# The beginning and the latent stage of a two-layer hybrid backbone: modulation weights in tiles that are written later, products in column groups, tokens first, projections reordered

## The chip, the cores and the metric

The kernel runs on one core of a Trainium2 chip. The metric is the device time of one execution in microseconds (us). A core has TensorE (matmuls, PE in the profile; its weight loads are PEld), VectorE (DVE), ScalarE (ACT), GpSimd (POOL) and SyncE (SP), each with its own queue of instructions that runs in order, and 16 DMA engines that move data between DRAM and the on-chip memory. Transfers are issued from the queues of SP, ACT and POOL.

## The reference

The reference is a backbone of two layers over 1024 latent tokens and 256 context tokens of width 1024. Each layer computes six modulation vectors from a conditioning vector (a product with `ada_w`), normalises and modulates the tokens, and mixes them. Layer 0 mixes by latent attention and a gated linear attention side by side, layer 1 by a gated delta rule; a squared-ReLU MLP follows in each. What the change touches is the head of layer 0:

```
ml = jnp.split(jax.nn.silu(c) @ ada_w[layer] + ada_b[layer], N_MOD, axis=-1)     # and mc from c_ctx
a_lat = modulate(rms_norm(h_lat, norm1_w[layer]), ml[0], ml[1])                  # h * (1 + scale) + shift
y = a_lat @ w_in                                                                 # split into cq, ckv, kpe, gq, ...
q = rms_norm(cq, q_norm) @ w_uq
kv = rms_norm(ckv, kv_norm) @ w_ukv                                              # k_nope and v of each head
```

The context tokens go the same way with `mc`. Rotary positions are applied to `kpe` and to a part of `q`, and eight heads attend over all 1280 tokens.

## The kernel before

Activations lie transposed: 128 features on the partitions, tokens along the free dimension, in eight feature tiles `xs` and in three token blocks of 512, 512 and 256 (`BLOCKS`). Every projection is done in three matmuls, because each operand is split in a high part (a cast to fp32r) and a low part (the rest): `mm3`, lines 181 to 183. `split` (lines 167 and 170) makes the parts: the cast on ACT, the subtraction on VectorE or POOL as its caller says. `load_w` (line 174) loads a weight tile `wst` on SP's queue and splits it into `whi` and `wlo`.

A scheduler sets the order on each engine from the order in which the code is written and from when it expects operands to be ready, so instructions that are written later can stand earlier. A tile that is given new contents waits for the last reader of the old ones. Generators put in `lanes` are advanced by `pump` while projections are written, so that their work lies beside these.

**The beginning** (lines 565 to 595). `ada_first(m, half, ...)`, lines 140 to 156, makes half of one modulation vector; in this text it is one unit. It loads eight weight tiles of 128x512 (256 KB) into a pool `adaw` of six buffers (line 146), multiplies each with the two conditioning columns `sc` into a PSUM tile `py` of 2 rows (line 147), copies `py` to `evt` (line 149), turns it over with four matmuls into `adat` (line 152), and adds the bias into `mod` (line 154). Vector 1 is the scale and gives `A` (line 161), vector 0 the shift. Written order: scale unit of the first half, `x` of block 0, shift unit of the first half, statistics of `x` (`sq`, line 238, summed on VectorE and POOL, line 243; `st`, line 252; root, lines 205 to 215), spread over the partitions as `rb` (line 261), and the weights of the first projections 0 and 1. Then come two halves of the eight feature tiles: normed and modulated into `a0h` and `a0l` (lines 281 to 288), multiplied for projections 0 and 1 of block 0. Before the second half stand the other two units and the loads of `x` for blocks 1 and 2. Projection 3 of block 0 is done by itself afterwards, beside the norm of block 1; then follow blocks 1 and 2 for all three.

**The latent stage** (lines 687 to 765). The projections 5 to 9 leave `cq` (three tiles) and `ckv` (two) in a long-lived pool with `small_t`. The stage loads the value weights in two tiles, splits all of `ckv` and then all of `cq` (line 716), applies the rotation to the shared key part (`kp`, `k2`, lines 722 to 730), then computes the values `pv` of ten token tiles (lines 737 to 739), copies each on ACT to `vo` (line 741) and stores it (line 742). Then the rotary parts of the queries are projected in two groups (`S` with `cqh`, `cql`; lines 181 to 183 again), rotated (lines 753 to 757), split into `peh` and `pel` (lines 758, 759) and stored by POOL (lines 761, 762). `gs` (line 487) is the tail of the linear attention, which still runs beside it. The attention's tiles get constant rows 96 from ACT (lines 779 to 782) and constant columns from VectorE (line 783). Its head projects keys and queries of a pair (`ckh`, `cqh`), finds the maxima by products `M` (line 857) and reductions `mx` (line 858), and then starts the scores.

## Time and profile before

| | |
|---|---|
| median of 3 runs | 3441.19 us (3430.4 to 3442.38) |
| time of the profiled execution | 3433.3 us |
| its span | 3431.6 us |
| mean granted TensorE clock | 0.971 |
| busy: PE, DVE, ACT, POOL | 95%, 62%, 34%, 30% |
| moved by DMA | 287.87 MB |

A row of the timeline has the start from the beginning of the span, the length of one instruction or of a merged group (xN), the engine, the line, the operation with output and inputs, and in brackets how long the engine had been idle and what ended that. A row of the waits has who waited for whom, the us in total, how often, and the longest. A row of the stretches has the busy time and count of PE, PEld, DVE, ACT and POOL, the granted clock, the share of the DMA engines and GB/s. The end of a matmul is modelled, and an f32 matmul is recorded as two; so the distance from one start to the next says more than its length.

### The profile page before, as it was taken

What the parts mean: (1) busy time and instruction counts of PE and PEld (TensorE: products, weight loads), DVE (VectorE), ACT (ScalarE), POOL (GpSimd) and SP (SyncE); (2) the same over time, 40 slices, a digit from 0 to 9 for tenths busy, and PEclk for the clock granted to TensorE, in tenths of its full rate; (3) what the DMA queues carried; (4) which work ended last, traced back from release to release, by engine and by line L of the source; (5) the groups of instructions that cost most, each with busy time, mean ns of one, the idle gap of its engine ahead of it and who ended that gap; (6) DMA issues with size and microseconds to landing.
All of it is one profiled execution on the core that took longest, in us unless ns stands there. A gap on an engine that the chain in (4) does not pass through costs nothing.

```text
span 3431.6 us, 48429 instructions
## 1 busy us (share of the span) xinstructions
PE 3261.4 (95%) x18676; PEld 2708.2 (79%) x18676; DVE 2114.5 (62%) x3888; ACT 1173.9 (34%) x2158; POOL 1045.7 (30%) x790
## 2 busy tenths in 40 slices
PE   8988889999899999999999998999999999999998
PEld 4876767777787888888888786777987788888887
DVE  4757536666467777777545779783765444444445
ACT  3234245666332111111211454552664311111112
POOL 2312136666221111111111343443117422212222
PEclk9998989999999999999999999999999999999999
DMA  5633133111523222222111244346454211111111
GB/s 198 199 100 90 59 111 81 30 37 39 178 69 94 82 77 82 77 79 82 50 37 37 74 105 102 84 121 154 106 108 148 68 49 49 44 50 49 44 49 62
DMA packets 284967, 287.87 MB, mean 84 GB/s; under 512 B 156424, under 2 KB 222032, under 8 KB 284736
## 3 DMA queue, kind: packets, MB, share of 16 engines
q1 hardware_dynamic: 272928, 263.53, 26.6%
q0 software_dynamic: 5760, 10.75, 1.3%
q10 hardware_dynamic: 6048, 10.49, 1.0%
q8 instruction: 147, 2.41, 0.3%
q14 instruction: 84, 0.69, 0.1%
HBM read 231.34 MB, written 53.36 MB: 83 GB/s over the span
## 4 chain that ended last, share of the span: by engine, by line
PE 58%; DVE 8%; issue 2%; ACT 2%; POOL 1%; DMA 1%; SPq 1%; DVEq 0%; ACTq 0%; POOLq 0%
PE ps L181 17%; PE ps L183 17%; PE ps L182 17%; DVE X L1399 1%; DVE tm L1397 1%; PE pa L1646 1%; PE pa L1618 1%; DVE acc L126 1%; PE pa L1629 1%; PE pb L1627 1%; PE pb L1667 1%; DVE y L1175 1%; DMA adaw<-in_adaw_dram 1%; PE adat L133 1%; PE st L252 0%
## 5 line engine op out<-in xcount | busy, mean ns | idle before, releaser
L170 POOL TENSOR_TENSOR wlo<-wst,whi 128x1024 fp32r<-128x1024 f32 (+1 forms) x192 | 453.2, 2368 | 1609.7 <-ACT whi L167 1549.3
L167 ACT CAST whi<-wst 128x1024 fp32r<-128x1024 f32 (+2 forms) x213 | 212.6, 1012 | 824.1 <-PE ps L182 766.4
L181 PE MATMUL ps<-th,whi 128*128 128x512 f32 (+1 forms) x1304 | 480.2, 368 | 5.0 <-DVE h L1070 3.4
L183 PE MATMUL ps<-th,wlo 128*128 128x512 f32 (+1 forms) x1304 | 476.9, 366 | 2.4 <-POOL wlo L170 2.4
L182 PE MATMUL ps<-tl,whi 128*128 128x512 f32 (+1 forms) x1304 | 477.9, 366 | 0.0
L1033 DVE TENSOR_TENSOR rl<-rl 128x512 f32<-128x512 f32 (+1 forms) x160 | 209.9, 1312 | 328.4 <-ACT rl L1032 328.0
L181 PE MATMUL ps<-mxh,whi 128*128 128x512 f32 (+1 forms) x1008 | 355.0, 353 | 0.0
L182 PE MATMUL ps<-mxl,whi 128*128 128x512 f32 (+1 forms) x1008 | 350.4, 348 | 0.9 <-POOL mxl L170 0.9
L183 PE MATMUL ps<-mxh,wlo 128*128 128x512 f32 (+1 forms) x1008 | 349.8, 347 | 0.0
L126 DVE SCALAR_TENSOR_TENSOR acc<-adaw,sc,acc 128x256 f32<-128x256 f32 (+1 forms) x476 | 277.1, 624 | 46.0 <-DMA adaw<-in_adaw_dram 46.0
L1070 DVE SCALAR_TENSOR_TENSOR h<-ps,mod,h 128x512 f32<-128x512 f32 (+1 forms) x384 | 243.2, 656 | 86.5 <-PE ps L183 85.1
L181 PEld LDWEIGHTS ps<-th,whi 128*128 128x128 f32 x1304 | 247.0, 189 | 49.0 <-DVE h L1070 5.3
L183 PEld LDWEIGHTS ps<-th,wlo 128*128 128x128 f32 x1304 | 246.7, 189 | 43.5 <-POOL wlo L170 3.2
L182 PEld LDWEIGHTS ps<-tl,whi 128*128 128x128 f32 x1304 | 247.2, 190 | 38.5
L1070 DVE SCALAR_TENSOR_TENSOR g<-ps,mod,g 128x512 f32<-128x512 f32 (+1 forms) x264 | 188.5, 731 | 106.3 <-PE ps L183 106.1
L182 PEld LDWEIGHTS ps<-mxl,whi 128*128 128x128 f32 x1008 | 193.3, 192 | 26.3 <-issue 1.4
L181 PEld LDWEIGHTS ps<-mxh,whi 128*128 128x128 f32 x1008 | 193.1, 192 | 26.1 <-issue 1.2
L183 PEld LDWEIGHTS ps<-mxh,wlo 128*128 128x128 f32 x1008 | 193.0, 192 | 23.4
L932 POOL TENSOR_TENSOR pl<-P,ph 128x512 fp32r<-128x512 f32 x144 | 179.3, 1252 | 90.1 <-DVE ph L931 58.1
L183 PE MATMUL ps<-m1h,wlo 128*128 128x512 f32 x512 | 203.9, 398 | 0.0
L181 PE MATMUL ps<-m1h,whi 128*128 128x512 f32 x512 | 203.8, 398 | 0.0
L182 PE MATMUL ps<-m1l,whi 128*128 128x512 f32 x512 | 203.7, 398 | 0.0
(376 smaller groups left out, 6747.0 us busy)
## 6 DMA issues: line engine op xcount, KB each, us to landing
wst<-in_w_dram SPq DMA_DIRECT2D x128, 512.0 KB, 3.6
adaw<-in_adaw_dram SPq DMA_DIRECT2D x224, 128.0 KB, 2.1
adaw<-in_adaw_dram SPq DMA_DIRECT2D x80, 256.0 KB, 5.3
wst<-in_owT_dram SPq DMA_DIRECT2D x25, 512.0 KB, 3.4
wst<-in_ewo_dram SPq DMA_DIRECT2D x16, 512.0 KB, 4.0
wY<-d_YA SPq DMA_DIRECT2D x64, 128.0 KB, 3.0
wst<-in_owo_dram SPq DMA_DIRECT2D x16, 512.0 KB, 3.5
wst<-in_ewT_dram SPq DMA_DIRECT2D x14, 512.0 KB, 7.3
```

The source lines that it names most:

```text
L126: V.scalar_tensor_tensor(out=acc[c], in0=w, scalar=sc[:, k, c:c + 1], in1=acc[c], op0=ALU.mult, op1=ALU.add)
L133: PE.matmul(pt[:, j, c:c + 1], acc[c][:, j * 128:(j + 1) * 128], ones, start=True, stop=True)
L167: S.copy(out=hi, in_=src)
L170: lo_eng.tensor_tensor(out=lo, in0=src, in1=hi.bitcast(F32), op=ALU.subtract)
L181: PE.matmul(ps, hi_w, hi_x, start=first, stop=False)
L182: PE.matmul(ps, hi_w, lo_x, start=False, stop=False)
L183: PE.matmul(ps, lo_w, hi_x, start=False, stop=last)
L932: (V if j % 4 == 3 else G).tensor_tensor(out=pl[:, :n], in0=P_[:, :n], in1=ph[:, :n].bitcast(F32), op=ALU.subtract)
L1033: V.tensor_tensor(out=r[:, :n], in0=r[:, :n], in1=r[:, :n], op=ALU.mult)
L1070: V.scalar_tensor_tensor(out=h[m][:, c0:c0 + n], in0=ps[:, :n], scalar=mod[l][:, 40 + m, c:c + 1], in1=h[m][:, c0:c0 + n], op0=ALU.mult, o ...
L1175: V.scalar_tensor_tensor(out=y[:, o0:o1], in0=src, scalar=cw[:, m, j:j + 1], in1=y[:, o0:o1], op0=ALU.mult, op1=ALU.add)
L1397: V.tensor_tensor(out=t3, in0=X[:, k + 1:, k:k + 1].to_broadcast([128, n, k]), in1=X[:, k:k + 1, :k].to_broadcast([128, n, k]), op=ALU.mult)
```

## The change

**Units.** `ada_load` (new) issues a unit's loads, into tiles of the long-lived pool that get their own contents only later: the first eight slots lie in `cq` and `ckv`, the other eight in `ckv`, `small_t` and, in two pieces of 256 columns each, in the columns of `xs` for block 2. The pool `adaw` goes. `ada_first` multiplies with `scz`, which is `sc` padded with zeros to 32 columns, and puts the eight products in turn into four groups of 32 rows of `py`, each at its own column group of the array (`tile_position`); the copy takes 128 rows, and a selector `sel` with two columns adds the groups up while it turns them over.

**Order of the beginning.** `x` of block 0 is loaded first, then the scale unit, the two weights, the shift unit and the third weight, which now has its pool early. The loads of the second half's units and of `x` for block 1 are written ahead of the first half. Projection 3 is done in the halves too, after 0 and 1. The statistics of block 1 come after the projections 0 and 1 of the second half, and its norm is run through before block 1.

TensorE at the start of the program, before: `py` are a unit's products, `adat` turns it over, `st` are the statistics of block 0, `rb` its spread root, `ps` the first projection.

```order
L147 MATMUL py<-adaw,sc 2x512 x8
L152 MATMUL adat<-ident,evt 128x2 x4
L147 MATMUL py<-adaw,sc 2x512 x8
L152 MATMUL adat<-ident,evt 128x2 x4
L252 MATMUL st<-ones,sq 128x1 x8
L147 MATMUL py<-adaw,sc 2x512
L261 MATMUL rb<-ident,rs_y 128x128 x4
L147 MATMUL py<-adaw,sc 2x512 x2
L181 MATMUL ps<-a0h_0_129,whi 128x512 x2
```

The same place after it:

```order
L158 MATMUL py<-cq_115,scz 32x512 x2
L158 MATMUL py<-cq_116,scz 32x512 x2
L158 MATMUL py<-cq_117,scz 32x512 x2
L158 MATMUL py<-ckv_118,scz 32x512 x2
L164 MATMUL adat<-sel,evt 128x2 x4
L264 MATMUL st<-ones,sq 128x1 x8
L273 MATMUL rb<-ident,rs_y 128x128 x4
L158 MATMUL py<-ckv_119,scz 32x512 x2
```

The statistics and the spread moved ahead of the second unit.

TensorE around the spread of block 1, before (`a0h_2` to `a0h_4` are feature tiles of block 0, here in projection 3):

```order
L183 MATMUL ps<-a0h_2_131,wlo 128x512
L261 MATMUL rb<-ident,rs_y 128x128 x4
L181 MATMUL ps<-a0h_3_132,whi 128x512
L182 MATMUL ps<-a0l_3_140,whi 128x512
L183 MATMUL ps<-a0h_3_132,wlo 128x512
L181 MATMUL ps<-a0h_4_133,whi 128x512
```

And after (`a0h_6` and `a0h_7` are the last feature tiles of block 0, `a0h_0_145` the first of block 1):

```order
L194 MATMUL ps<-a0l_6_143,whi 128x512
L195 MATMUL ps<-a0h_6_135,wlo 128x512
L193 MATMUL ps<-a0h_7_136,whi 128x512
L194 MATMUL ps<-a0l_7_144,whi 128x512
L195 MATMUL ps<-a0h_7_136,wlo 128x512
L273 MATMUL rb<-ident,rs_y 128x128 x4
L193 MATMUL ps<-a0h_0_145,whi 128x512 x2
```

Fifteen products of block 0 stood between the spread and block 1; now none does.

**Latent stage.** The weight pool `wa` has three buffers and is made ahead of the split tiles. The value weights are loaded without being split at once: first block 0 of `ckv` is split, then the weights, one on VectorE and one on POOL, then the rest of `ckv`, all low parts on VectorE. The splits of `cq` are written one by one between the value products. Every other copy `vo` is on VectorE. The constant rows of `Kh` and `Ql` are copied by POOL, those of `Kl` stay on ACT.

VectorE at the start of the latent stage, before (`kp`, `k` are the rotation, `ckl` and `cql` low parts, `gs` the tail of the linear attention):

```order
L722 TENSOR_TENSOR kp<-small_t,cosT 32x512
L487 SCALAR_TENSOR_TENSOR gs<-pt,gon,gs 128x512
L170 TENSOR_TENSOR ckl_3729<-ckv_118,ckh_3724 128x512
L723 TENSOR_TENSOR k_3790<-small_t,sinT 32x512
L170 TENSOR_TENSOR ckl_3729<-ckv_118,ckh_3724 128x512
L170 TENSOR_TENSOR ckl_3729<-ckv_118,ckh_3724 128x256
```

After (`wlo` is the low part of the first value weights, `vo` the copy of the first value tile):

```order
L754 TENSOR_TENSOR kp<-small_t,cosT 32x512
L182 TENSOR_TENSOR ckl_3715<-ckv_118,ckh_3713 128x512
L499 SCALAR_TENSOR_TENSOR gs<-pt,gon,gs 128x512
L182 TENSOR_TENSOR wlo<-wst,whi 128x512
L755 TENSOR_TENSOR k_3761<-small_t,sinT 32x512
L182 TENSOR_TENSOR ckl_3715<-ckv_118,ckh_3713 128x512
L182 TENSOR_TENSOR ckl_3716<-ckv_119,ckh_3714 128x512
L182 TENSOR_TENSOR ckl_3715<-ckv_118,ckh_3713 128x256
L182 TENSOR_TENSOR ckl_3716<-ckv_119,ckh_3714 128x256
L755 TENSOR_TENSOR k_3772<-small_t,sinT 32x512
L754 TENSOR_TENSOR kp<-small_t,cosT 32x512
L776 COPY vo<-pv 128x512
```

The weights' low part came to VectorE, behind `gs`; the low parts of the second `ckv` tile came from POOL in the later blocks.

Within the attention a few rows change places; after it the order of instructions is the same in both kernels on every engine.

```diff
--- before.py
+++ after.py
@@ -137,19 +137,31 @@
                 if m == src:
                     ada_scales(l, which)
 
-    def ada_first(m, half, wpool, ypool, ppool):
+    def ada_load(m, half, ws):
+
+        u = 2 * m + half
+        for k in range(KD):
+            c = u * 512
+            for w in ws[k]:
+                nc.sync.dma_start(out=w, in_=a["adaw"][0, k * 128:(k + 1) * 128, c:c + w.shape[1]])
+                c += w.shape[1]
+
+    def ada_first(m, half, ws, sel, ypool, ppool):
+
 
         u = 2 * m + half
         py = ppool.tile([128, 512], F32, name="py", tag="q")
         for k in range(KD):
-            w = wpool.tile([128, 512], F32, name="adaw", tag="adaw")
-            nc.sync.dma_start(out=w, in_=a["adaw"][0, k * 128:(k + 1) * 128, u * 512:(u + 1) * 512])
-            PE.matmul(py[:2], sc[:, k, :], w, start=(k == 0), stop=(k == KD - 1))
+            z = 32 * (k % 4)
+            c = 0
+            for w in ws[k]:
+                PE.matmul(py[z:z + 32, c:c + w.shape[1]], sel[1][:, k, :], w, start=(k < 4), stop=(k >= 4 and w is ws[k][-1]), tile_position=(0, z))
+                c += w.shape[1]
         y = ypool.tile([128, 512], F32, name="evt", tag="evt")
-        V.tensor_copy(out=y[:2], in_=py[:2])
+        V.tensor_copy(out=y, in_=py)
         pt = ppool.tile([128, 4, 2], F32, name="adat", tag="q")
         for j in range(4):
-            PE.matmul(pt[:, j, :], y[:2, j * 128:(j + 1) * 128], ident[:2, :2], start=True, stop=True)
+            PE.matmul(pt[:, j, :], y[:, j * 128:(j + 1) * 128], sel[0], start=True, stop=True)
         us = slice(u * 4, u * 4 + 4)
         V.tensor_tensor(out=mod[0][:, us, :], in0=pt, in1=adab[:, 0, us].unsqueeze(2).to_broadcast([128, 4, 2]), op=ALU.add)
         if m == 1:
@@ -563,33 +575,46 @@
             first = [(0, to_sb(small_t)), (1, to_dram(d_gq[0])), (3, to_dram(d_gk[0]))]
             pq = pool(e2, "ppq", 3, space=PSUM)
             e3 = ExitStack()
-            aw = pool(e3, "aw0", 6)
-            ada_first(1, 0, aw, evp, pq)
+            wx = pool(e2, "wx", 1)
+            sx = pool(e3, "sx")
+            sel = (sx.tile([128, 2], F32, name="sel"), sx.tile([128, KD, 32], F32, name="scz"))
+            V.tensor_reduce(out=sel[0], in_=ident.rearrange("p (g c) -> p c g", c=32)[:, 0:2, :], axis=AX.X, op=ALU.add)
+            V.memset(sel[1], 0.0)
+            V.tensor_copy(out=sel[1][:, :, 0:2], in_=sc)
+
+            late = [[x[:, j * 512:(j + 1) * 512]] for x in cq + ckv + [small_t] for j in range(2)]
+            late += [[xs[k][:, 1024:], xs[k + 1][:, 1024:]] for k in range(0, KD, 2)]
+            late = [late[:8], late[8:]]
             load_x(0)
-            ada_first(0, 0, aw, evp, pq)
+            ada_load(1, 0, late[0])
+            ada_first(1, 0, late[0], sel, evp, pq)
+            ws0 = [load_w(a["ewT"][m], wp) for m in (0, 1)]
+            ada_load(0, 0, late[1])
+            ws0.append(load_w(a["ewT"][3], wx))
             r0 = run(stat_lane(xs, c0, n, tmp, small, pq, "q", D))
             rb = spread(r0, n // 128, pp, "p")
-            ws0 = [load_w(a["ewT"][m], p) for m, p in ((0, wp), (1, wp))]
-            pss = [pp.tile([128, 512], F32, name="ps", tag="p") for _ in range(2)]
+            ada_first(0, 0, late[1], sel, evp, pq)
+            ada_load(1, 1, late[0])
+            ada_load(0, 1, late[1])
+            load_x(1)
+            pss = [pp.tile([128, 512], F32, name="ps", tag="p") for _ in range(3)]
             for half in range(2):
+                ks = range(4 * half, 4 * half + 4)
                 if half:
-                    ada_first(1, 1, aw, evp, pq)
-                    load_x(1)
-                    ada_first(0, 1, aw, evp, pq)
+                    ada_first(1, 1, late[0], sel, evp, pq)
+                    ada_first(0, 1, late[1], sel, evp, pq)
                     load_x(2)
-                    r1 = run(stat_lane(xs, 512, 512, tmp, small, pq, "q", D))
-                run(norm0(0, rb=rb, ks=range(4 * half, 4 * half + 4)))
-                for k in range(4 * half, 4 * half + 4):
-                    for w, ps in zip(ws0, pss):
-                        mm3(ps[:, :n], *colk(w, k), *a0.at(k, c0, n), k == 0, k == KD - 1)
+                run(norm0(0, rb=rb, ks=ks))
+                for ms in ((0, 1), (2,)):
+                    for k in ks:
+                        for m in ms:
+                            mm3(pss[m][:, :n], *colk(ws0[m], k), *a0.at(k, c0, n), k == 0, k == KD - 1)
+                    if half and 0 in ms:
+                        r1 = run(stat_lane(xs, 512, 512, tmp, small, pq, "q", D))
             e3.close()
-            wx = pool(e2, "wx", 1)
-            ws0.append(load_w(a["ewT"][3], wx))
             for (_, dst), ps in zip(first, pss):
                 dst(c0, n, ps)
-            nl = lane(norm0(1, r=r1))
-            dense0(first[2:], BLOCKS[:1], 0.8, 1.6, None, ws0[2:])
-            complete(nl)
+            complete(lane(norm0(1, r=r1)))
             lane(norm0(2))
             dense0(first, BLOCKS[1:2], 0.8, 1.6, None, ws0)
             drain()
@@ -685,12 +710,12 @@
 
 
     el = ExitStack()
+    wp = pool(el, "wa", 3)
     hip = pool(el, "hip")
+    ckh = [hip.tile([128, T], F32R, name=f"ckh{i}") for i in range(2)]
+    ckl = [hip.tile([128, T], F32R, name=f"ckl{i}") for i in range(2)]
     cqh = [hip.tile([128, T], F32R, name=f"cqh{i}") for i in range(3)]
-    ckh = [hip.tile([128, T], F32R, name=f"ckh{i}") for i in range(2)]
     cql = [hip.tile([128, T], F32R, name=f"cql{i}") for i in range(3)]
-    ckl = [hip.tile([128, T], F32R, name=f"ckl{i}") for i in range(2)]
-    wp = pool(el, "wa", 2)
     def proj(m, nm, kt, xh, xl, w, pp, tag):
 
         hi, lo = w
@@ -709,12 +734,19 @@
         nc.scalar.dma_start(out=sinT, in_=a["sinT"])
         tmp = pool(e2, "tmpq", 2)
         pp = pool(e2, "ppq", 4, space=PSUM)
-        wv = [load_w(a["ukvv"][:, k * 512:(k + 1) * 512], wp, 512) for k in range(2)]
-
-        for hs, hh, hl in ((ckv, ckh, ckl), (cq, cqh, cql)):
-            for (c0, n) in BLOCKS:
-                for i, x in enumerate(hs):
-                    split(x[:, c0:c0 + n], hh[i][:, c0:c0 + n], hl[i][:, c0:c0 + n], (V, G)[i % 2])
+        sts = []
+        for k in range(2):
+            sts.append(wp.tile([128, 512], F32, name="wst", tag="wst"))
+            nc.sync.dma_start(out=sts[k], in_=a["ukvv"][:, k * 512:(k + 1) * 512])
+        wv = []
+        for (c0, n) in BLOCKS:
+            for i, x in enumerate(ckv):
+                split(x[:, c0:c0 + n], ckh[i][:, c0:c0 + n], ckl[i][:, c0:c0 + n], V if c0 else (V, G)[i % 2])
+            if not c0:
+                for k in range(2):
+                    wv.append(tuple(wp.tile([128, 512], F32R, name=x, tag=x) for x in ("whi", "wlo")))
+                    split(sts[k], *wv[k], (V, G)[k])
+        later = [(cq[i][:, c0:c0 + n], cqh[i][:, c0:c0 + n], cql[i][:, c0:c0 + n], (V, G)[i % 2]) for c0, n in BLOCKS for i in range(3)]
         for (c0, n) in BLOCKS:
             cs = slice(c0, c0 + n)
             kp, k2 = (tmp.tile([32, 512], F32, name=x, bufs=1)[:, :n] for x in ("kp", "k2"))
@@ -738,7 +770,12 @@
                 PE.matmul(ps, ckh[k][:, x0], wvl, start=False, stop=False)
                 PE.matmul(ps, ckl[k][:, x0], wvh, start=False, stop=(k == 1))
             vo = tmp.tile([128, 512], F32, name="vo")
-            S.copy(out=vo, in_=ps)
+            if t % 2:
+                S.copy(out=vo, in_=ps)
+            else:
+                V.tensor_copy(out=vo, in_=ps)
+            if later:
+                split(*later.pop(0))
             nc.sync.dma_start(out=d_v[t * 128:(t + 1) * 128, :], in_=vo)
             pump(1.3)
 
@@ -776,10 +813,10 @@
     identr = at.tile([128, 128], F32R, name="identr")
     S.copy(out=identr, in_=ident)
     for i in range(3):
-        S.copy(out=Kh[i][96:97, :], in_=ident[96:97, 96:97].to_broadcast([1, T]))
+        G.tensor_copy(out=Kh[i][96:97, :], in_=ident[96:97, 96:97].to_broadcast([1, T]))
         S.activation(out=Kl[i][96:97, :], in_=ident[96:97, 96:97].to_broadcast([1, T]), func=AF.Copy, scale=0.0)
         for q in Ql[i]:
-            S.activation(out=q[96:97, :], in_=ident[96:97, 96:97].to_broadcast([1, q.shape[1]]), func=AF.Copy, scale=0.0)
+            G.tensor_copy(out=q[96:97, :], in_=ident[96:97, 0:1].to_broadcast([1, q.shape[1]]))
         V.tensor_copy(out=Vh[i][:, :, 64:128], in_=ones.unsqueeze(1).to_broadcast([128, NT, 64]))
 
         G.dma_start(out=Kh[i][64:96, :], in_=d_kp[0])
```

## The prediction

> **What bounds the kernel now.** I read the page first, then who waits for whom on TensorE, then the timeline of the two places that the change touches, then busy time by stretches.
>
> ```profile
> span 3431.6 us, 48429 instructions
> PE 3261.4 (95%) x18676; PEld 2708.2 (79%) x18676; DVE 2114.5 (62%) x3888; ACT 1173.9 (34%) x2158; POOL 1045.7 (30%) x790
> ```
>
> TensorE is busy for 95%, so some 170 us are all that reordering can win anywhere. The profiled execution took 3433.3 us, 1.7 beyond its span and 7.9 below the median of the three runs (3441.19). Half a per cent, 17.2 us, is about what a measurement of this kernel can tell from no change. TensorE's waits that lie in the two places, in us, times and longest:
>
> ```profile
> PE rb L261 <- DVE rs_y L215: 11.3, 6, 3.8
> PE py L147 <- DMA adaw<-in_adaw_dram: 7.1, 2, 6.1
> PE pv L737 <- ACT ckh L167: 6.7, 1, 6.7
> PE pv L737 <- ACT vo L741: 4.7, 2, 3.6
> PE S L181 <- ACT whi L167: 3.8, 1, 3.8
> ```
>
> The last three, 15.2 us, belong to the latent stage. In the beginning little of the loss is a listed wait: there TensorE is busy with slow `py` products while the first projections wait behind them. The timeline (start, length, engine, line):
>
> ```profile
> 6.13 9.98 PE L147 MATMUL py<-adaw,sc 128*2 128x512 f32 x16 [6.13 <-DMA adaw<-in_adaw_dram]
> 15.46 3.98 ACT L238 ACTIVATE sq<-x 128x512 f32<-128x512 f32 x6 [1.47 <-DMA x<-in_xT_dram]
> 29.64 1.95 PE L252 MATMUL st<-ones,sq 128*128 128x1 f32 x16
> 31.62 0.16 DVE L205 TENSOR_SCALAR rs_m<-st 128x4 f32<-128x4 f32 x1 [1.71 <-PE st L252]
> 34.32 2.08 PE L261 MATMUL rb<-ident,rs_y 128*128 128x128 f32 x8 [1.78 <-DVE rs_y L215]
> 39.66 0.73 PE L181 MATMUL ps<-a0h,whi 128*128 128x512 f32 x2
> 46.16 0.39 PE L183 MATMUL ps<-a0h,wlo 128*128 128x512 f32 x1
> 50.11 0.68 DVE L149 COPY evt<-py 2x512 f32<-2x512 f32 x1 [0.20 <-PE py L147]
> 50.84 1.05 PE L152 MATMUL adat<-ident,evt 2*128 2x2 f32 x8 [0.77 <-DVE evt L149]
> 51.82 7.03 PE L147 MATMUL py<-adaw,sc 128*2 128x512 f32 x16
> 60.71 0.17 DVE L154 TENSOR_TENSOR mod<-adat,adab 128x8 f32<-128x8 f32 x1 [1.14 <-PE adat L152]
> 60.91 0.72 ACT L284 ACTIVATE a0h<-nt,mod 128x512 fp32r<-128x512 f32 x1 [11.64 <-DVE mod L154]
> 62.41 0.71 PE L181 MATMUL ps<-a0h,whi 128*128 128x512 f32 x2
> 74.80 1.06 PE L261 MATMUL rb<-ident,rs_y 128*128 128x128 f32 x8
> 79.21 0.39 PE L181 MATMUL ps<-a0h,whi 128*128 128x512 f32 x1
> ```
>
> Four marks count: H1 (39.66, first half of the first projections begins), E1 (46.55, it ends), H2 (62.41, second half begins) and B1 (79.21, token block 1 begins). From B1 on the work is the same in both kernels, so what B1 moves, the end moves. The chain to H1 ran statistics (29.64), root (31.62 to 34.32: 2.7), spread (34.32); E1 to H2 is two modulation units one after the other.
>
> **The beginning, worked.** Tokens come first now, then the scale unit of the first half. In the trace the sixteenth 256 KB tile is the last of `x`; the six squares end at 19.44, so it was there by 18.8. Now the sixteenth tile is the last of that unit: 18.8. Then 0.9 for its last product, 0.72 for the copy `evt` (50.11 to 50.84), 1.1 for `adat`, 1.95 for `st`, 2.7 for the root, 2.1 for `rb`: 28.3. The shift unit comes behind 1.05 MB of projection weights, 3.15 MB in all, at the rates (last column, GB/s) of a fed queue:
>
> ```profile
> 10.00:15.00 5.00, 5.00 (x10) 0.88 (x9) 0.00 (x0) 1.26 (x2) 0.00 (x0) 1.00 0.97 336
> 15.00:20.00 5.00, 2.74 (x12) 1.13 (x11) 3.85 (x7) 3.76 (x6) 2.95 (x3) 0.89 1.04 382
> ```
>
> This takes 8.2 to 9.4 us, so it lands at 27.0 to 28.2, just hidden; were its smaller 128x256 pieces slower by half, some 2 us would show.
>
> The products in column groups do not occur before. The nearest row is `pk`, on quarter tiles of the array, against whole-array matmuls of the same length:
>
> ```profile
> 243.23 1.10 PE L435 MATMUL pk<-gvt,gkn 64*64 64x128 f32 x32
> 458.34 1.05 PE L656 MATMUL ps<-ident,rs_y 128*128 128x128 f32 x8
> ```
>
> That is 0.034 against 0.131 us each, 3.8 times as many. I take 3, since 32-column groups all read 128 rows: a unit (7.03 us at full clock) costs P = 2.3 us. Bounds: 1.8 (the full 3.8), and 9.98, the row at the beginning at half clock with no overlap. The Trainium skill, "TensorE: Matmul & The Clock Gate", Part 3, reports 2.38 times for three column tiles of 32 over 512 columns; by that P would be an estimated 3.0 and the sum 2 us worse. No run here shows column groups alone yet.
>
> The clock: between `rb` (74.80, 0.9 to its last start) and B1 lie fifteen matmul records, 0.23 us each at full clock. After a long wait they are slower, and the latent stage shows how long:
>
> ```profile
> 472.15 0.62 ACT L167 CAST whi<-wst 128x512 fp32r<-128x512 f32 x1 [4.34 <-DMA wst<-in_ukvv_dram]
> 472.86 0.75 DVE L487 SCALAR_TENSOR_TENSOR gs<-pt,gon,gs 128x512 f32<-128x512 f32 x1 [2.21 <-DMA gs<-d_gs]
> 473.34 0.79 PE L737 MATMUL pv<-whi,ckh 128*128 128x512 f32 x1 [6.73 <-ACT ckh L167]
> 479.59 0.47 PE L738 MATMUL pv<-wlo,ckh 128*128 128x512 f32 x1
> 482.91 4.88 DVE L170 TENSOR_TENSOR cql<-cq,cqh 128x512 fp32r<-128x512 f32 x5
> 488.32 2.35 DVE L783 CAST Vh<-ones 128x640 fp32r<-128x640 f32 x3
> 491.50 0.79 PE L737 MATMUL pv<-whi,ckh 128*128 128x512 f32 x1 [3.56 <-ACT vo L741]
> 493.26 0.41 POOL L726 COPY kp<-small_t 32x256 f32<-32x256 f32 x1
> 498.27 0.50 PE L181 MATMUL S<-cqh,whi 128*128 128x512 f32 x1
> 512.79 0.50 PE L181 MATMUL S<-cqh,whi 128*128 128x512 f32 x1 [3.76 <-ACT whi L167]
> 517.24 0.42 PE L183 MATMUL S<-cqh,wlo 128*128 128x512 f32 x1
> 525.11 0.40 PE L181 MATMUL S<-ckh,whi 128*128 128x512 f32 x1
> 540.71 0.43 DVE L836 SCALAR_TENSOR_TENSOR Ql<-S,Qh 64x256 fp32r<-64x256 f32 x1 [1.75 <-ACT Qh L835]
> ```
>
> After 6.7 us of waiting, records are slow from 473.34 to 479.59: 13 of them (two output tiles and one) in 6.25 us, 3.3 more than at full clock. After 3.8 us it is from 512.79 to 517.24, 4.45 us, of which about half, 2.2, is lost. The same page, Part 1, says that some 3.4 us of activity bring the full clock back; by it a stretch would cost an estimated 1.7. The trace has 4.5 to 6.3 here, and I go by the trace.
>
> H1: the shift unit runs from 28.3, in part cold, 3.4; copy, `adat`, `mod` and the first ACT step add 0.72 + 1.1 + 0.2 + 0.75: H1 = 34.5, against 39.66. E1: the third projection is in the half now, 36 records and one product instead of 24; 13 cold in 6.25, 24 at 0.23: 11.8, so 46.3. E1 to H2: two units, 2 x 2.3, two copies with `adat`, 2 x 1.82, and 0.95: 9.2, so H2 = 55.5. H2 to B1: 36 records, 11.55, and `st`, 1.95, bring 69.0; but the spread of block 1, which lay under the third projection, is now alone: a PSUM copy (0.7) that stands ahead of the root's last two steps (0.35), `rb` 0.85, the first norm 0.7, ACT 0.75: 3.35, so 72.35, and that idle time makes block 1 start cold, 2.7 (between 2.2 and 3.3). Taken together 75.0 against 79.21: **-4.2 us**. Bounds: without the three cold stretches (9.3) and at P = 1.8 (1.6 and twice 0.5), -16.1; at P = 9.98 each (6.6 and twice 7.7), +17.8.
>
> The evicted copy is 128 partitions instead of 2, at no cost (columns set it); the selector and padded weights are made on VectorE while it is idle before the first `x`. All landing tiles are written by their owners only later. The second half's loads wait in SP's queue for TensorE's reads, done at 19.7 and 31.7, and `x` of block 1 waits behind them; at about 6 us for 2.1 MB they land by 36, 42 and 48 (third weight 1.5 first), and are wanted at E1, E1 + 4 and after H2.
>
> **The latent stage, worked.** ACT now casts `ckh` ahead of the value weights, so two products run at once, but the low part of the first weights is on VectorE behind `gs`, which ends at 473.6: 474.7, where the same products began at 473.34. So this wait stays. Then 58 records: 13 cold to 480.95; 21 more to 485.8, the end of the sixth tile. The seventh needs the third tile's copy, on VectorE behind 13 operations (0.98 each by the row of 4.88 for five), 487.4, plus 0.7: a wait of 2.3. The ninth needs the fifth's, behind two splits 1.6, a weight split 0.55 and the casts of ones 2.35: 493.3, a wait of 2.4. The end is 496.1 against 498.27: -2.2. In the query projections the wait of 3.76 goes, since ACT has twelve copies fewer ahead of the weights and a third buffer lets these land early, and with it the cold stretch, 2.2: -5.9. In the attention's start the cast of `vf` no longer stands ahead of the last `Qh`: -1.75. Sum **-9.9 us**. Bounds: -15 without the two copy waits, -3 if one copy wait goes cold and the attention gains nothing.
>
> The copies moved to POOL: 0.41 us for 256 columns gives 2.0, 0.8, 0.8 and 0.4 a head, 12 us in all. They stand ahead of the loads of `Kh` and the stores of `peh`, which the maximum products wait for. Cover is POOL's idle time there (sixth figure: 1.97 of 10):
>
> ```profile
> 500.00:510.00 10.00, 9.03 (x49) 7.63 (x47) 4.68 (x7) 7.92 (x12) 1.97 (x4) 1.00 0.68 192
> ```
>
> At twice the price this would still fit; without the cover, 12 us would be late.
>
> The sum is -14.1: 3419.2 beside the profiled 3433.3, and 3427.1 beside the median: **3427 us**.
>
> **The rivals.** *Warm beginning* (-28 us, 3413): short waits between the units keep the clock up, so the three cold stretches go (-13.5 there), and VectorE's splits take 0.75 rather than 0.98, so that no copy is waited for (-15). For it: from H1 to E1 of the trace 24 records took 6.9 us, 0.28 each, after mixed work. Against it: from H2 to B1 48 records, `rb` and `st` took 16.8. The skill's rule of 3.4 us leans this way; from that alone the estimate would be some 4 us better.
>
> *Column groups do not overlap* (slower, 3449): place, the four units; price, P = 9.98 instead of 3.4 and twice 2.3, +22 us, so the sum is +7.9. It turns slower than before from P = 7.4. For it: no row has 32-column groups, and both halves of an f32 product go to the same group. Against it: `pk` has the same pairs. The Trainium skill, "TensorEngine Tiling (Array Packing)", Key Properties, says that a change of tiling mode drains TensorE; that leans this way, but the 1.10 us of `pk`, which stands between whole-array products, hold whatever it costs.
>
> *VectorE inherits the latent stage* (3436): it now makes all later `ckl`, one weight split and half the copies. At an estimated 1.65 us an operation, two thirds above the row, the seventh tile waits 8.7 us longer; the sum is -5. For it: 0.98 is a mean over 512 and 256 columns, and already above the 0.75 of `gs`. Against it: POOL, which worked beside it there, has no more to split than before.
>
> **The numbers.** Chances: forecast 0.42, warm beginning 0.33, VectorE 0.15, no overlap 0.10. Faster by over 17.2 us: nearly all of the warm case and the better quarter of the forecast, 0.43; slower by as much: only the far end of no overlap, 0.03; within: 0.54. The range: both lower bounds together give -31.1, 3410, less 2 for the runs' spread of 12 us: 3408; upward it holds the VectorE case and ends at no change, 3441; left out are no overlap and the ends.
>
> **What would show it.** Right: H1 near 34.5, units of 2 to 3 us on TensorE, H2 near 55, a gap of some 3 us before B1, no wait of `S` for `whi`, two waits of `pv` for VectorE's copies. Wrong: units of 7 us or more; H2 after 60; `pv` ending after 498; maximum products waiting for POOL's transfers.

## The result and the profile after

The changed kernel takes 3420.96 us (median of 7 runs, 3413.66 to 3426.37) against 3439.51 for the kernel before (7 runs timed beside them, 3430.4 to 3446.0). The ratio is 0.995, 95% interval 0.9938 to 0.9963: 17 us faster, between 13 and 21, which is about the half per cent that can be told from no change. The prediction was 3427 (3408 to 3441): 14.1 below the median then known, 3441.19. The page of the changed kernel:

```profile
span 3416.7 us, 48479 instructions
PE 3241.0 (95%) x18692; PEld 2705.0 (79%) x18692; DVE 2116.7 (62%) x3899; ACT 1162.3 (34%) x2141; POOL 1051.5 (31%) x799
```

The span is 14.9 us shorter. TensorE is busy 20.4 us less and idle 5.5 us more, so on balance slow products are gone, and not waits. Lines have moved: `py` is now line 158, `rb` 273, the first projections 193 to 195, `pv` 769 to 771, copies of values 774 (ACT) and 776 (VectorE). Who waits for whom on TensorE:

```profile
PE py L158 <- DVE sq L255: 13.1, 1, 13.1
PE rb L273 <- DVE rs_y L227: 12.0, 9, 3.9
PE pv L770 <- DVE wlo L182: 4.4, 1, 4.4
PE pv L769 <- DVE vo L776: 4.2, 1, 4.2
PE pv L769 <- ACT whi L179: 2.9, 1, 2.9
```

The wait of `S` for `whi` (3.76) is gone; `pv` waits 11.5 us in three pieces where it waited 6.7 and 4.7. The 13.1 us are new only in part: the first unit stands behind the loads of `x` now, and TensorE's first product starts at 13.11 us, where it started at 6.13. The beginning in the timeline of TensorE:

```profile
28.36 1.07 PE L158 MATMUL py<-ckv,scz 128*32 128x512 f32 x2
30.07 1.95 PE L158 MATMUL py<-x,scz 128*32 128x256 f32 x16
35.09 0.83 PE L193 MATMUL ps<-a0h,whi 128*128 128x512 f32 x2 [1.01 <-ACT a0h L296]
46.29 1.48 PE L158 MATMUL py<-cq,scz 128*32 128x512 f32 x9
50.05 0.62 PE L158 MATMUL py<-ckv,scz 128*32 128x512 f32 x2
50.93 1.08 PE L158 MATMUL py<-x,scz 128*32 128x256 f32 x16
55.34 1.07 PE L193 MATMUL ps<-a0h,whi 128*128 128x512 f32 x3 [1.01 <-ACT a0h L296]
65.18 2.15 PE L264 MATMUL st<-ones,sq 128*128 128x1 f32 x14 [0.35 <-POOL sq L255]
70.73 2.08 PE L273 MATMUL rb<-ident,rs_y 128*128 128x128 f32 x8 [1.05 <-DVE rs_y L227]
74.47 1.22 PE L193 MATMUL ps<-a0h,whi 128*128 128x512 f32 x2 [1.66 <-ACT a0h L296]
80.64 0.40 PE L194 MATMUL ps<-a0l,whi 128*128 128x512 f32 x1
```

The shift unit starts at 28.36, the marks are H1 = 35.09, E1 = 46.29, H2 = 55.34, B1 = 74.47. A unit lasts 3.66 us at half clock (28.36 to 32.02) and 1.96 at full clock (50.05 to 52.01). B1 comes after two waits, and the records stay long up to 80.64 (0.44 us from one to the next, for 0.23 at full clock). The same stretch by windows (TensorE's busy time first, its granted clock third from the end):

```profile
65.00:70.00 5.00, 4.50 (x19) 3.49 (x19) 1.47 (x9) 0.00 (x0) 0.13 (x1) 0.63 0.49 161
70.00:75.00 5.00, 2.61 (x9) 2.28 (x10) 2.73 (x7) 1.31 (x2) 0.00 (x0) 0.50 0.14 52
75.00:80.00 5.00, 4.99 (x12) 3.05 (x11) 4.86 (x7) 4.28 (x8) 2.58 (x2) 0.50 0.00 0
```

TensorE is busy half of the second window. The granted clock falls in the first, ahead of both waits, and is 0.50 in the other two. The latent stage of the changed kernel, all engines:

```profile
465.22 1.27 POOL L182 TENSOR_TENSOR ckl<-ckv,ckh 128x512 fp32r<-128x512 f32 x1 [33.38 <-ACT ckh L179]
465.87 1.22 PE L769 MATMUL pv<-whi,ckh 128*128 128x512 f32 x2 [2.88 <-ACT whi L179]
467.31 0.67 DVE L182 TENSOR_TENSOR ckl<-ckv,ckh 128x512 fp32r<-128x512 f32 x1
469.53 0.75 DVE L499 SCALAR_TENSOR_TENSOR gs<-pt,gon,gs 128x512 f32<-128x512 f32 x1 [1.55 <-DMA gs<-d_gs]
471.53 0.80 PE L770 MATMUL pv<-wlo,ckh 128*128 128x512 f32 x1 [4.44 <-DVE wlo L182]
478.30 1.78 DVE L182 TENSOR_TENSOR cql<-cq,cqh 128x512 fp32r<-128x512 f32 x1
479.50 3.41 POOL L182 TENSOR_TENSOR cql<-cq,cqh 128x512 fp32r<-128x512 f32 x2
480.41 4.72 DVE L182 TENSOR_TENSOR cql<-cq,cqh 128x512 fp32r<-128x512 f32 x3
485.06 0.67 DVE L776 COPY vo<-pv 128x512 f32<-128x512 f32 x1
485.78 0.51 PE L769 MATMUL pv<-whi,ckh 128*128 128x512 f32 x1 [4.22 <-DVE vo L776]
492.99 0.39 PE L193 MATMUL S<-cqh,whi 128*128 128x512 f32 x1
513.64 0.40 PE L193 MATMUL S<-ckh,whi 128*128 128x512 f32 x1
532.97 0.76 PE L193 MATMUL S<-Qh,Kh 97*128 97x512 f32 x1 [0.77 <-ACT Qh L902]
```

The waits of 4.44 and 4.22 sit where two were predicted, behind `gs` and behind VectorE's splits; the third that was predicted did not come. To see how much of the gain each part has, I follow four marks in every trace: G, the first product `pa` of the gated attention, which has the same wait in both kernels:

```profile
236.20 4.71 PE L417 MATMUL pa<-gq,gk 64*128 64x128 f32 x40 [5.63 <-DVE gk L374]
```

```profile
232.10 4.71 PE L429 MATMUL pa<-gq,gk 64*128 64x128 f32 x40 [5.63 <-DVE gk L386]
```

then the end of the value products (first `S<-cqh`), the end of the query projections (first `S<-ckh`) and the first scores (`S<-Qh`). Before and after, in us:

| mark | before | after | shift | share since the mark before |
|---|---|---|---|---|
| G | 236.20 | 232.10 | -4.1 | beginning -4.1 |
| value products end | 498.27 | 492.99 | -5.3 | -1.2 |
| query projections end | 525.11 | 513.64 | -11.5 | -6.2 |
| first scores | 546.36 | 532.97 | -13.4 | -1.9 |

The rest of the 14.9, 1.5 us, came after the first scores, where the order of instructions is the same. That is within the spread of single traces: over all kernels of this document the time from the first scores to the end of the span, with the same order there, lies between 2881.1 and 2889.5 us.

### The profile page after: what moved, and what is told of

Read it like the earlier page. It is cut to its first block, busy times and chain, and to the rows that moved or that the text cites. A ratio compares the mean times of both kernels' runs of the same rounds, so it can differ in the third digit from the quotient of the medians.

```text
span 3416.7 us, 48479 instructions
## 1 busy us (share of the span) xinstructions
PE 3241.0 (95%) x18692; PEld 2705.0 (79%) x18692; DVE 2116.7 (62%) x3899; ACT 1162.3 (34%) x2141; POOL 1051.5 (31%) x799
## 3 DMA queue, kind: packets, MB, share of 16 engines
q1 hardware_dynamic: 274080, 263.53, 26.8%
## 4 chain that ended last, share of the span: by engine, by line
PE 59%; DVE 8%; ACT 2%; issue 2%; DMA 1%; SPq 1%; POOL 1%; DVEq 0%; ACTq 0%; POOLq 0%
PE ps L193 17%; PE ps L195 17%; PE ps L194 17%; DVE X L1436 1%; DVE tm L1434 1%; PE pa L1683 1%; PE pa L1655 1%; DVE acc L126 1%; PE pa L1666 1%; PE pb L1704 1%; PE pb L1664 1%; DVE y L1212 1%; DMA adaw<-in_adaw_dram 1%; PE adat L133 1%; PE st L264 0%
## 5 line engine op out<-in xcount | busy, mean ns | idle before, releaser
L182 POOL TENSOR_TENSOR wlo<-wst,whi 128x1024 fp32r<-128x1024 f32 (+2 forms) x191 | 451.3, 2370 | 1586.1 <-ACT whi L179 1549.3
```

Of the source, the lines that this page charges most:

```text
L182: lo_eng.tensor_tensor(out=lo, in0=src, in1=hi.bitcast(F32), op=ALU.subtract)
```

## The experiments

Twelve kernels beside the changed one, each timed against the kernel before on its chip. The last three columns are from each kernel's one trace: G, the query projections (first `S<-cqh` to first `S<-ckh`), and from G to the first scores.

| kernel | median us | ratio to before, 95% interval | G | query | G to scores |
|---|---|---|---|---|---|
| before | 3433.63 to 3439.51 | 1 | 236.2 | 26.8 | 310.2 |
| changed | 3420.96 | 0.995 (0.9938 to 0.9963) | 232.1 | 20.7 | 300.9 |
| beginning alone | 3427.55 | 0.9976 (0.9965 to 0.9987) | 232.3 | 26.2 | 310.8 |
| latent stage alone | 3424.36 | 0.9964 (0.995 to 0.9978) | 236.4 | 20.7 | 300.8 |
| one column group | 3431.70 | 0.9986 (0.9975 to 0.9998) | 242.2 | 20.7 | 300.7 |
| third projection last | 3423.45 | 0.9961 (0.9946 to 0.9976) | 234.4 | 20.7 | 303.1 |
| rows on ACT | 3421.65 | 0.9964 (0.9951 to 0.9976) | 232.3 | 20.7 | 300.9 |
| two buffers | 3421.06 | 0.9965 (0.9952 to 0.9978) | 233.6 | 22.4 | 302.6 |
| both | 3419.21 | 0.9955 (0.994 to 0.9969) | 233.4 | 22.2 | 302.3 |
| both, and copies on ACT | 3423.60 | 0.9961 (0.9947 to 0.9975) | 231.1 | 22.8 | 303.6 |
| copies on ACT | 3422.56 | 0.9964 (0.9951 to 0.9978) | 231.4 | 21.0 | 302.0 |
| low parts swapped | 3423.55 | 0.9969 (0.9957 to 0.9981) | 230.6 | 20.8 | 302.4 |
| two key buffers | 3421.68 | 0.9965 (0.9951 to 0.9979) | 230.5 | 20.7 | 301.9 |
| spread early | 3412.55 | 0.9941 (0.9924 to 0.9958) | 224.5 | 20.7 | 303.1 |

Kernels with the same beginning have G between 230.5 and 233.6, so a shift of 1.5 us in one trace says little. The intervals of the ratios overlap too, the changed kernel's with all but those of "beginning alone" and "one column group"; where the clock does not separate two kernels, I go by the traces.

**The two parts alone.** The edits are the hunks of the diff up to line 620 of the changed kernel, and those behind it.

> The kernel before with the beginning of the change alone; the latent stage is as it was. Theory (each part is worth what its marks in the trace of after moved): the first product of the gated attention came 4.1 us earlier (236.20 to 232.10), so the time falls by 4.1 us, between 2.5 and 6; against the kernel before a ratio of 0.9988. Rival (the two parts help each other, or something outside both moved): the medians fell by 18.5 us while the marks show 13.4 up to the first scores; then this part alone would give 8 us or more.

> The kernel before with the latent stage of the change alone; the beginning is as it was. Theory: the marks of the stage moved by 1.2 us to the end of the value products, 6.2 more to the end of the query projections and 1.9 more to the first scores, so the time falls by 9.3 us, between 7.5 and 11.5; the wait of the query projections for their weights (3.76) is gone here too. Rival: part of it is owed to the earlier beginning (loads that stand otherwise in their queue), and this part alone gives 6 or less; or, with the beginning at 4, what remains up to 18.5 lies here and it gives 14.

By the marks both theories hold: G comes 3.9 earlier with the beginning alone and not at all with the latent stage alone, which shortens the way from G to the first scores by 9.4. The wait of `S` for `whi` stays with the beginning alone (3.8 in two pieces) and is absent with the latent stage alone. By the clock, the latent stage gives 12 us (8 to 17), in agreement. The beginning gives 8 (4.5 to 12), more than its 4.1: by the clock the rival's "8 or more" fits better, though the interval also holds the upper end of the theory. The trace places no more than 4, so some 4 us of that are not placed.

**What the column groups are worth.**

```diff
-            z = 32 * (k % 4)
+            z = 0
...
-start=(k < 4), stop=(k >= 4 and w is ws[k][-1])
+start=(k == 0), stop=(k == KD - 1 and w is ws[k][-1])
...
```

The copy `evt` and the selector take 32 rows accordingly.

> The changed kernel, with all sixteen products of a modulation unit in one column group, one after the other, in place of four groups at a time; landing tiles, order and padded columns stay. Theory (the overlap of the groups is what makes the units short, 1.9 to 2.0 us in the second half): a unit takes 7 to 10 us again; the two of the second half cost 5 to 8 more each, the shift unit of the first half 6 more, the scale unit up to 4 more behind the last load, and the time rises by 16 to 24 us over the changed kernel, which is slower than the kernel before by 0 to 6 us. Rival (the units were bound by their loads, and the groups are worth little beside the earlier loads): it rises by less than 8 us.

TensorE's timeline: two pieces of units that stand elsewhere than in the changed kernel, then one whole unit, the last:

```profile
27.03 3.62 PE L158 MATMUL py<-ckv,scz 128*32 128x512 f32 x4
39.61 1.90 PE L158 MATMUL py<-cq,scz 128*32 128x512 f32 x4
57.58 1.90 PE L158 MATMUL py<-ckv,scz 128*32 128x512 f32 x4
59.33 1.88 PE L158 MATMUL py<-small_t,scz 128*32 128x512 f32 x4
61.04 3.62 PE L158 MATMUL py<-x,scz 128*32 128x256 f32 x16
```

```profile
242.22 4.70 PE L429 MATMUL pa<-gq,gk 64*128 64x128 f32 x40 [5.62 <-DVE gk L386]
```

The unit takes 7.08 us (57.58 to 64.66) against 1.96: 3.6 times. G comes 10.1 later than in the changed kernel and 6.0 later than before the change: without the groups this beginning loses. (The whole kernel is still 5 us, 1 to 9, faster than before by the clock, since its latent stage is the changed one.) The cost is 10 and not 16 to 24. Part of the difference is that the scheduler put the first 3.6 us of the shift unit into the wait for the root (from 27.03) and 1.9 us of the next unit into the wait before the first projections (from 39.61), where the theory had all of it on the path. The rival had less than 8, so the mechanism is the theory's and the size lies between.

**The wait before block 1.** B1 came 2.1 us later than predicted, behind two waits. First attempt: the third projection as before, by itself after the halves.

```diff
-            pss = [pp.tile([128, 512], F32, name="ps", tag="p") for _ in range(3)]
+            pss = [pp.tile([128, 512], F32, name="ps", tag="p") for _ in range(2)]
...
-                for ms in ((0, 1), (2,)):
+                for ms in ((0, 1),):
...
-            complete(lane(norm0(1, r=r1)))
+            nl = lane(norm0(1, r=r1))
+            dense0(first[2:], BLOCKS[:1], 0.8, 1.6, None, ws0[2:])
+            complete(nl)
```

> The changed kernel, with the third projection of token block 0 taken out of the two halves and made by itself after them, as in the kernel before, so that statistics and norm of block 1 lie beside it. Theory (the idle time before block 1, 1.05 and 1.66 us, and the stretch at half clock behind it, 74.5 to 80.6, come from the third projection no longer covering them): both go, and the time falls by 4 to 6 us below the changed kernel. Rival (the cover is only moved: the second half then begins with TensorE idle for 2.8 us longer, since its modulation units wait for their loads or because VectorE has not ended its work): within 1.5 us of the changed kernel.

```profile
72.65 2.08 PE L273 MATMUL rb<-ident,rs_y 128*128 128x128 f32 x8 [1.05 <-DVE rs_y L227]
76.39 1.22 PE L193 MATMUL ps<-a0h,whi 128*128 128x512 f32 x2 [1.66 <-ACT a0h L296]
```

Both waits are there to the hundredth, and G is 2.3 later. The scheduler took the third projection's products as filler earlier, between the modulation units: all 72 products of block 0 were done before `rb`. The second half begins 2.0 later (57.34), with products standing ahead of it and not idle, as the rival had it. My theory of the cover fell. What the two kernels share is that `st` comes at 65 to 67, since the squares of block 1 stand on ACT behind the norm of the second half, and their last sums, on GpSimd, behind them (rows of the changed kernel):

```profile
60.00 5.12 POOL L255 TENSOR_TENSOR sq<-sq 128x512 f32<-128x512 f32 x3
61.78 1.18 ACT L250 ACTIVATE sq<-x 128x512 f32<-128x512 f32 x2 [0.52 <-POOL sq L255]
```

So the second attempt moves squares, sums and spread ahead:

```diff
                     load_x(2)
+                    r1 = run(stat_lane(xs, 512, 512, tmp, small, pq, "q", D, engs=(G, G)))
...
-                        r1 = run(stat_lane(xs, 512, 512, tmp, small, pq, "q", D))
+                        rb = spread(r1, 4, pp, "p")
...
-            complete(lane(norm0(1, r=r1)))
+            complete(lane(norm0(1, rb=rb)))
```

> The changed kernel, with the statistics of block 1 written ahead of the norm of block 0's second half (its sums on GpSimd alone), and its spread written ahead of the third projection's last products. Theory (the idle time before block 1 comes from the squares of block 1, which stand on ACT behind the norm of the second half and are added up at 59 to 65 us; what the third projection does cannot cover it): the waits of 1.05 and 1.66 before block 1 go, and most of the half clock behind them (74.5 to 80.6), so that the first product of the gated attention comes 3 to 6 us earlier than 232.1 and the time falls by as much below the changed kernel. Rival (the sums and x of block 1 are too late even so, and the second half now begins later by what the first products wait for the statistics): within 1.5 us, or later.

```profile
53.57 2.29 PE L264 MATMUL st<-ones,sq 128*128 128x1 f32 x16
64.26 1.05 PE L273 MATMUL rb<-ident,rs_y 128*128 128x128 f32 x8
224.46 4.71 PE L429 MATMUL pa<-gq,gk 64*128 64x128 f32 x40 [5.63 <-DVE gk L386]
```

`st` stands at 53.57 in a wait that was idle, `rb` at 64.26 without a wait, and the longest wait left between H2 (55.72) and 75 is 0.32. G comes 7.6 us earlier, a little more than the theory's 6. Of that, 5.4 are left at the first scores (527.53): 2.2 are lost again up to the end of the value products, where the stage itself was not edited, and no run tells why. The time is 3412.55, 20 us (14 to 26) below before: the lowest ratio here. Its interval overlaps the changed kernel's, which was timed apart; the two kernels timed together with it, "both" and "two key buffers", have the changed beginning and took 3419.21 and 3421.68, 7 to 9 more, with other edits in the latent stage.

**What took the wait for `whi` away.** The prediction said: ACT's twelve copies fewer, and the third buffer.

```diff
-        G.tensor_copy(out=Kh[i][96:97, :], in_=ident[96:97, 96:97].to_broadcast([1, T]))
+        S.copy(out=Kh[i][96:97, :], in_=ident[96:97, 96:97].to_broadcast([1, T]))
...
-    wp = pool(el, "wa", 3)
+    wp = pool(el, "wa", 2)
```

The first (with the rows of `Ql` likewise) is "rows on ACT", the second "two buffers".

> The changed kernel, with the constant rows of Kh and Ql back on ACT. Theory (as predicted: the query projections' wait of 3.76 us for their weights went because ACT has twelve copies fewer ahead of the casts of these weights): that wait comes back, 3 to 4 us with 2 us of half clock behind it, and the time rises by 4 to 7 us over the changed kernel. Rival (the third buffer took the wait away): within 1.5 us of the changed kernel, no wait of S for whi.

> The changed kernel, with two buffers of weights in the latent stage in place of three. Theory (ACT's shorter queue took the wait away, the third buffer helps little): within 1.5 us of the changed kernel. Rival (the third buffer did it): the casts wait for TensorE's last reads of the pair before, which in the trace of before ended at 508.75 with the products starting again at 512.79, and 3 to 6 us come back.

With the rows back there is no such wait at all: the theory that the rows were the cause is wrong by itself. With two buffers the projections take 1.7 more, short of the rival's 3 (there `S` waits 0.8 and 0.2 for VectorE's `wlo`, not for `whi`). Then both together:

> The changed kernel, with both taken back that could have removed the query projections' wait: the constant rows are on ACT again and the weights have two buffers. Each alone left the wait away. Theory (either one suffices: a free buffer lets the casts start early past a long queue, and a short queue lets them start at once when the buffer comes free): the wait of S for whi comes back, 3 to 4 us with 2 us of half clock, and the query projections take 25 us or more from the end of the value products, where the changed kernel takes 20.65 and the one before 26.84; the time rises by 4 to 7 us. Rival (neither took it away, but the copies of values and the cast of Vh that no longer stand there): 22.5 us or less, and the time rises by 2 or less.

```profile
505.24 0.50 PE L193 MATMUL S<-cqh,whi 128*128 128x512 f32 x1 [0.79 <-ACT whi L179]
```

The wait is 0.79, the rival's case: neither of the two that I named is what counts. Last, the copies of values back on ACT as well (the diff is below):

> The changed kernel, with three reliefs of ACT taken back at once: the constant rows are on ACT, all ten copies of the value products are on ACT, and the weights of the latent stage have two buffers. With the first and the third taken back, the query projections waited 0.8 us for their weights and took 22.2 us from the end of the value products. Theory (the wait of 3.76 went because ACT's whole queue between the value products and the casts of the second pair of query weights became shorter, so that several reliefs stand in for each other): now that these casts stand in ACT's order behind all rows of the third head and both tiles of scaled products, the wait of S for whi is 3 us or more, with half clock behind it, and the projections take 25 to 27.5 us; the time is 4 to 7 us above the changed kernel. Rival (the copies are no part of it; the earlier casts of the query latents or the order of the weights' loads took it away): the wait stays under 1.5 us and the projections take 22.5 or less.

```profile
504.17 0.50 PE L193 MATMUL S<-cqh,whi 128*128 128x512 f32 x1 [1.75 <-DVE pel L793]
```

A wait of 1.75 (the profile names `pel`, but ACT's cast of `whi`, from 503.62, ended at about the same time) and 22.8 us, where before took 26.8: between the two, nearer to the rival. All three reliefs together explain 2.1 of the 6.2 us. The other 4.1 belong to what is left of the rewrite, such as the new order of casts and loads around the value products; which part it is stays open, and was not tried. The traces give a hint only: before the change, ACT reached these casts 14.0 us after the query projections began (512.25), behind constant rows and a copy of values that had waited 1.9 for a store; with all three reliefs undone it reached them after 11.7.

**What holds the value products.**

```diff
-            if t % 2:
-                S.copy(out=vo, in_=ps)
-            else:
-                V.tensor_copy(out=vo, in_=ps)
+            S.copy(out=vo, in_=ps)
```

> The changed kernel, with all ten copies of the value products on ACT, none on VectorE. Theory (the wait of 4.2 us at the seventh tile is VectorE's queue of splits, which take 1.6 to 1.8 us each while GpSimd works too): the wait goes, with the half clock behind it, and the time falls by 3 to 6 us below the changed kernel. Rival (ACT's casts of the latents stand ahead of the copies in its queue, as before the change, where two waits made 4.7 us): within 1.5 us of the changed kernel.

```profile
487.67 0.40 ACT L179 CAST kph<-kp 32x256 fp32r<-32x256 f32 x1 [3.27 <-DMA d_kp<-kph]
488.60 0.58 PE L769 MATMUL pv<-whi,ckh 128*128 128x512 f32 x1 [4.42 <-ACT vo L773]
```

The wait goes from VectorE's queue (4.2) to ACT's (4.4), where the copy stands behind a cast of keys that waits for a store from its only buffer, and not behind the casts of the latents that the rival named. With two buffers for them, beside copies on ACT:

> The changed kernel, with all copies of the value products on ACT and two buffers instead of one for the high and low parts of the rotated keys. Theory (with the copies on ACT the wait of 4.4 at a late tile stayed because in ACT's queue the copy stands behind the cast of the last rotated keys, idle for 3.3 us until the store of the ones before has left their only buffer): the wait falls to 1.5 us or less, the value products end 3 to 5 us earlier, and the time falls by 2 to 5 below the changed kernel. Rival (another item of ACT's queue is late next, the operand of that cast that GpSimd makes, or the store of the copies): the wait is still 3 or more and the time within 1.5 us of the changed kernel.

```profile
485.39 0.40 ACT L179 CAST kph<-kp 32x256 fp32r<-32x256 f32 x1 [3.68 <-POOL kp L758]
487.95 0.80 PE L769 MATMUL pv<-whi,ckh 128*128 128x512 f32 x1 [4.98 <-ACT vo L773]
```

Now the same cast waits for GpSimd, which makes its operand behind its own share of the splits; the rival holds. Last, the first wait of the stage:

```diff
-                    split(sts[k], *wv[k], (V, G)[k])
+                    split(sts[k], *wv[k], (G, V)[k])
```

> The changed kernel, with the low part of the first value weight on GpSimd and that of the second on VectorE. Theory (the low part of the first waits on VectorE behind gs, which waits for its load; 4.4 us): three products run some 3 us earlier, but the fifth waits for the second weight's low part behind the same gs, at about 471; the time falls by 0.5 to 2 us. Rival (the second weight's load, landed at 469.0, sets the point): 0, within 0.5 us.

```profile
PE pv L769 <- DVE vo L776: 5.7, 2, 4.9
PE pv L770 <- DVE wlo L182: 1.5, 1, 1.5
PE pv L770 <- POOL wlo L182: 1.5, 1, 1.5
```

The first wait shrinks from 4.4 to two of 1.5, the wait for the copies grows from 4.2 to 5.7, and the value products end no earlier: 262.4 us after G, for 260.9. So the theory's 0.5 to 2 did not come. In each of these traces the copy that is waited for stands behind splits, on VectorE or by way of GpSimd. I read this as a stage whose splits fill the three engines together, so that an edit at one of them only renames the wait; no run took splits out, so this is not shown.

## Why the prediction came out right

**The beginning: -4.2 predicted, -4.1 at G.** Shift unit 28.3 predicted, 28.36 in the trace; H1 34.5 and 35.09; E1 46.3 and 46.29; H2 55.5 and 55.34. The units, whose overlap no row showed, took 3.66 at half and 1.96 at full clock for 3.4 and 2.3. The Trainium skill, "TensorE: Matmul & The Clock Gate", Part 3, has 2.38 times for three column tiles, which had given an estimated P of 3.0. The 3.6 times measured here for four decide.

That the numbers agree so closely is in part luck. The statistics began 0.7 earlier than summed (20.85), and from there to `rb` took 0.85 longer. B1 came at 74.47 for 72.35. The wait ahead of `rb` came as counted (1.05), but the clock was at half from the statistics of block 1 on, where I had full clock: `rb` took 2.08 for 0.85, the products and `st` ahead of it 14.3 for 13.5, the wait behind it 1.7 for 1.45. Against this, block 1 lost less than I charged. Its half clock itself cost 2.9 (14 records in the 6.2 us from 74.47), for 2.7; but otherwise block 1 took 1.7 less than in the kernel before, which the sum had not counted, so that up to the first 256-column products of block 2 the lead shrank by only 1.2, from 4.7 to 3.5. These rows are from before and after:

```profile
99.29 0.28 PE L181 MATMUL ps<-a0h,whi 128*128 128x256 f32 x1
95.77 0.28 PE L193 MATMUL ps<-a0h,whi 128*128 128x256 f32 x1
```

From there to G it grew by 0.6 again. The Trainium skill, "TensorE: Matmul & The Clock Gate", Part 1, has 3.4 us of activity to full clock; here the stretch from 74.47 lasted 6.2 and the one from 55.34 some 4.3, about as long as those in the trace of before (6.25 and 4.45), and these decide.

**The latent stage: -9.9 predicted, -9.3 from G to the first scores.** Value products -2.2 predicted, -1.2 measured from G; counted from the stage's own start (the end of the work before it, 466.6 before and 463.0 after) it is -1.7. The parts were off by more. Counted from the stage's start, the resumption at 471.53 is 0.5 later than the 474.7 of the sum; the products from there to the sixth tile took 1.2 less, since fewer of them were slow; and one wait of 4.2, with 1.7 of half clock behind it, stands for two of 2.3 and 2.4 without. The seventh tile's copy stood behind splits of 1.57 to 1.78 us, not 0.98. That is the price of the rival *VectorE inherits the latent stage* (1.65), though only for the last four, so that the stage still gained. Query projections -5.9 predicted, -6.2 measured: right in size, and wrong in its reason as far as the runs show, since the rows and the third buffer that I named bring back 1.5 of it when both are undone. Attention's start -1.75 predicted, -1.9 measured, and as predicted: the cast of `vf` stands behind the last `Qh` now.

**The rivals.** *Column groups do not overlap* is refuted by the unit of 1.96, and the run with one group shows that its other half was true: with no overlap the beginning loses 6.0 against before at G. Its price was misread, though. The 9.98 that I called a unit at half clock is no such row: the granted clock over it is 1.00. In the run with one group the unit takes 7.08 at full clock, and four records take 3.62 at a granted clock of 0.51 (from 27.03) for 1.90 at full, so at half clock a whole unit would be an estimated 13.5. The reason against the rival had a slip as well: the neighbours of `pk` in the trace of before are products over 32 rows (242.18 and 244.26), and not whole-array products. *Warm beginning* did not come either: the three half-clock stretches, from H1, H2 and B1, are in the trace.

**The size.** The trace gave 14.9 of span for the 14.1, and the timed runs 17 (13 to 21). The remainder over the marks showed up with the beginning alone, and no trace places it.

## What to carry over

Where a scheduler fills idle time by itself, a wait is removed by making its operand early, not by leaving work beside it: with squares and spread moved ahead the first scores came 5.4 us earlier, with the products moved they came 4.5 later. When a predicted gain arrives in the right size, undo its named cause alone before believing it; here most of the gain in the query projections had another cause. In a stage where three engines share one row of small operations, moving one of them to another engine renamed the wait in each of the three runs; what is left to try is taking work out of the stage.

## What the runs showed of the hardware

A subtraction of 128x512 on VectorE took 0.67 us with GpSimd idle (467.31) and 1.57 to 1.78 while GpSimd was at work on subtractions and on the keys' rotation (478.30 and 480.41). GpSimd's own went from 1.27 with VectorE idle (465.22) to 1.7 each (479.50). So one on each engine took about 1.65 us beside each other, where two on VectorE alone would take an estimated 1.34 by the row of 0.67. By these rows the split over two engines gained nothing there; no run gave all of it to VectorE. Four column groups of 32 gave 3.6 times in a unit of f32 products over 512 and 256 columns.
